# Moving GpSimd's candidate sums of the product-key search to between the two halves of the next head's scores

## The chip, the cores and the metric

The kernel runs on one core of one Trainium2 chip. The metric is the device time of one execution in microseconds (us): the median of three runs before the change is 2715.93 us (2709.26 to 2721.87). A core has TensorE (PE in the profile), VectorE (DVE), ScalarE (ACT), GpSimd (POOL) and SyncE (SP, which here issues most of the DMAs). Each engine works through its own instructions in the order in which they were put there and waits at an instruction whose input is not ready.

## The reference

The program is two transformer blocks on 512 tokens of width 1024. The change lies in the last part of the second block, a memory layer that looks up experts by product keys:

```python
def chunk(xc):
    q = (xc @ wq).reshape(PEER_CHUNK, PEER_HEADS, 2, half)
    s1 = jnp.einsum('chd,hnd->chn', q[:, :, 0], keys1)
    s2 = jnp.einsum('chd,hnd->chn', q[:, :, 1], keys2)
    v1, i1 = lax.top_k(s1, 16)
    v2, i2 = lax.top_k(s2, 16)
    cand = (v1[..., :, None] + v2[..., None, :]).reshape(..., 256)
    cidx = (i1[..., :, None] * 128 + i2[..., None, :]).reshape(..., 256)
    best, pos = lax.top_k(cand, 16)
    eidx = jnp.take_along_axis(cidx, pos, axis=-1)
    g = jax.nn.softmax(best, axis=-1)
    a = jnp.einsum('chkd,cd->chk', u_tab[eidx], xc)
    wgt = gelu(a) * g
    return jnp.einsum('chk,chkd->cd', wgt, v_tab[eidx])
```

Every token has 8 heads. A head has two halves of 128 scores each; the 16 largest of each half are added pairwise, and the 16 largest sums choose 16 of 16,384 experts.

## The kernel before, in words

`peer` (L1395) treats three of the four groups of 128 tokens densely: all 128 blocks of `u_tab` are multiplied with those 384 tokens on TensorE (`u_chunk`, L1422), and the chosen experts' weights are then picked from the result. The fourth group fetches its 128 rows of `u_tab` and `v_tab` per token by indirect DMA (`gather`, L1478; `use`, L1498).

The stage around the change is the search, L1514 to L1612. The loop at L1605 goes over the 8 heads and is one head ahead with its scores: `scores(h + 1)` is called before `best16(h)`.

`scores(h)` (L1522) does the following for each half: it loads a tile of 128x1024 of the query weights and splits it into a high and a low part (`wload`, L72: ScalarE makes the high part at L69, GpSimd the low part at L70); 24 matmuls of 512 columns make the queries (`mm3`, L87 to L89); ScalarE copies them (L1534); four small matmuls with the keys make the scores (L1538), which ScalarE copies to `sk` (L1540); VectorE takes the 16 largest of each of the four token groups with `top16` (L1385: the values at L1388 and L1392 into the tile `tkv`, the indices at L1389 and L1393 into `tki`). Then `ahead(1)` (L1436) puts one `u_chunk` behind it: another split by ScalarE and GpSimd, 24 matmuls of 384 columns, and a Gelu on ScalarE (L1430). Such blocks give TensorE work while VectorE searches.

`best16(h, val, ixu)` (L1546) begins with four GpSimd additions (L1551) that make the 80 candidate sums which can be among the 16 largest (`cand`). VectorE takes their 16 largest (L1557, again `top16`, tile `best`), ScalarE makes the softmax (L1563, L1565), and VectorE turns the positions back into expert indices (the decode, L1576 to L1601, with ScalarE's copies at L1572, L1587, L1599 and L1602). For odd heads, `ahead(h % 2)` adds one more block (L1559). After it the loop calls `gather(2)` from the second head on: GpSimd issues two indirect DMAs (L1493) and multiplies two rows that came earlier (L1503). Before `best16(7)` there are four more blocks, `ahead(TRANS)`, L1608.

What sets the order: for GpSimd, the order of this stage is that of the program text (`manual_schedule`, L1474). For the other engines a scheduler of the framework, which simulates the program as it is written down, chooses the order of instructions. So GpSimd's queue before the change is, for head h of the loop: split of half 0 of head h+1, split of a block, split of half 1 of head h+1, split of a block, the four sums of head h, (odd h: split of a block), two indirect DMAs with two multiplications. The tile `whi` has three buffers, `acc` two, `cand` two, `tkv` three.

Of the kernel before, what the change touches and what calls it, by code (L numbers as in the profile page):

```python
# [9 lines left out]
F32 = mybir.dt.float32  # L10
# [6 lines left out]
ALU = mybir.AluOpType  # L17
# [6 lines left out]
NT = S // 128  # L24
# [22 lines left out]
class Emit:  # L47
# [1347 lines left out]
    def peer(self):  # L1395
        tc, nc, A = self.tc, self.nc, self.A
# [8 lines left out]
        with ExitStack() as es:  # L1405
# [108 lines left out]
            with ExitStack() as ek:  # L1514
                pv = ek.enter_context(tc.tile_pool(name="pval", bufs=1))
                slot = pv.tile([128, 3, ND, 128], F32, name="slot")
                i16 = pv.tile([128, 2, 16], F16, name="i16")
                for half in range(2):
                    nc.gpsimd.iota(i16[:, half], pattern=[[1 + 3 * half, 16]], base=0, channel_multiplier=0,
                                   allow_small_or_imprecise_dtypes=True)  # L1520
                pk = ek.enter_context(tc.tile_pool(name="pk", bufs=2))
                def scores(h):  # L1522
                    val = pk.tile([128, NT, 2, 16], F32, name="tkv", bufs=3)
                    ixu = pk.tile([128, NT, 2, 16], U32, name="tki", bufs=3)
                    keys = pk.tile([128, 256], F32, name="keys")
                    self.dma(keys, A["pkeys"][h])
                    for half in range(2):
                        wh, wl = self.wload(A["pwq"][2 * h + half], eng=nc.gpsimd if h >= 0 else None)
                        ps = self.acc()
                        for k in range(KD):  # L1530
                            c = slice(k * 128, k * 128 + 128)
                            self.mm3(ps, wh[:, c], wl[:, c], hh[:, k], hl[:, k], k == 0, k == KD - 1)
                        q = pk.tile([128, S], F32, name="pq")
                        nc.scalar.activation(q, ps, AF.Copy)  # L1534
                        p3 = self.bank()
                        for t in range(NT):
                            c = slice(t * 128, t * 128 + 128)
                            mm(p3[:, c], lhsT=q[:, c], rhs=keys[:, half * 128:half * 128 + 128], start=True, stop=True)  # L1538
                        sk = pk.tile([128, NT, 128], F32, name="sk")
                        nc.scalar.activation(sk, p3.rearrange("p (t n) -> p t n", t=NT), AF.Copy)  # L1540
                        for t in range(NT):
                            self.top16(pk, sk[:, t], 128, val[:, t, half], ixu[:, t, half])
                        ahead(1)
                    return val, ixu

                def best16(h, val, ixu):  # L1546


                    cand = pk.tile([128, NT, 80], F32, name="cand")
                    for o, i0, ni, nj in BLOCKS:  # L1550
                        nc.gpsimd.tensor_tensor(  # L1551
                            cand[:, :, o:o + ni * nj].rearrange("p t (i j) -> p t i j", i=ni),
                            val[:, :, 0, i0:i0 + ni, None].to_broadcast([128, NT, ni, nj]),
                            val[:, :, 1, None, 0:nj].to_broadcast([128, NT, ni, nj]), op=ALU.add)
                    best = pk.tile([128, NT, 16], F32, name="best")
                    pos = pk.tile([128, NT, 16], U32, name="pos")
                    for t in range(NT):  # L1557
                        self.top16(pk, cand[:, t], 80, best[:, t], pos[:, t])
                    ahead(h % 2)  # L1559
                    g = pk.tile([128, NT, 16], F32, name="gslot")  # L1560
                    mx = pk.tile([128, NT], F32, name="bmx")
                    nm = pk.tile([128, NT], F32, name="bnm")
                    nc.scalar.activation(nm, best[:, :, 0], AF.Copy, scale=-1.0)  # L1563
                    for t in range(NT):
                        nc.scalar.activation(g[:, t], best[:, t], AF.Exp, bias=nm[:, t:t + 1],  # L1565
                                             accum_out=mx[:, t:t + 1])
                    nc.vector.reciprocal(mx, mx)
                    hs = slice(h * 16, h * 16 + 16)
                    tt(slot[:, 2, :, hs], g[:, :ND], mx[:, :ND, None].to_broadcast([128, ND, 16]), op=ALU.mult)
                    tt(gg[:, hs], g[:, ND], mx[:, ND:NT].to_broadcast([128, 16]), op=ALU.mult)  # L1570
                    kf = pk.tile([128, NT, 2, 16], F16, name="kfl")
                    nc.scalar.activation(kf, ixu, AF.Copy)  # L1572


                    u = [pk.tile([128, NT, 16], U32, name=f"pu{i}", bufs=1) for i in range(3)]
                    ts(u[0], pos, 2, 0x3c, op0=ALU.logical_shift_left, op1=ALU.bitwise_and)  # L1576
                    ts(u[0], u[0], 0x40, None, op0=ALU.bitwise_or)
                    ts(u[1], pos, 4, 7, op0=ALU.logical_shift_right, op1=ALU.bitwise_xor)
                    tt(u[2], u[0], u[1], op=ALU.logical_shift_right)
                    tt(u[1], u[2], u[1], op=ALU.logical_shift_left)  # L1580
                    tt(u[0], u[0], u[1], op=ALU.bitwise_xor)
                    ts(u[0], u[0], 0x3c, None, op0=ALU.bitwise_and)
                    e = pk.tile([128, 2, NT, 16], F32, name="e12")
                    for half in range(2):

                        pu = pk.tile([128, NT * 16, 2], F16, name=f"pu2{half}")
                        nc.scalar.activation(pu, (u[0] if half else u[2]).rearrange("p t k -> p (t k)")[:, :, None]  # L1587
                                             .to_broadcast([128, NT * 16, 2]), AF.Copy)
                        eq = pk.tile([128, NT * 16, 16], F16, name="eq", bufs=2)
                        tt(eq.rearrange("p n (i j) -> p n i j", j=2), pu[:, :, None].to_broadcast([128, NT * 16, 8, 2]),  # L1590
                           i16[:, half].rearrange("p (i j) -> p i j", j=2)[:, None].to_broadcast([128, NT * 16, 8, 2]),
                           op=ALU.is_equal)
                        eq4 = eq.rearrange("p (t k) i -> p t k i", t=NT)
                        tt(eq4, eq4, kf[:, :, half, None, :].to_broadcast([128, NT, 16, 16]), op=ALU.mult)

                        for n in (8, 4):
                            tt(eq[:, :, 0:n], eq[:, :, 0:n], eq[:, :, n:2 * n], op=ALU.add)
                        red(e[:, half].rearrange("p t k -> p (t k)"), eq[:, :, 0:4], axis=AX.X, op=ALU.add)
                    nc.scalar.activation(slot[:, 0:2, :, hs], e[:, :, :ND], AF.Copy)  # L1599
                    ef = pk.tile([128, 16], F32, name="ef")  # L1600
                    stt(ef, e[:, 0, ND], 128.0, e[:, 1, ND], op0=ALU.mult, op1=ALU.add)  # L1601
                    nc.scalar.activation(ei[:, hs], ef, AF.Copy)  # L1602

                cur = scores(0)
                for h in range(8):  # L1605
                    nxt = scores(h + 1) if h < 7 else None
                    if h == 7:
                        ahead(TRANS)  # L1608
                    best16(h, *cur)
                    if h:  # L1610
                        gather(2)
                    cur = nxt  # L1612
                for t in range(ND):
                    c = slice(t * 32, t * 32 + 32)
                    p = self.bank()
                    for j in range(3):
                        nc.tensor.transpose(p[:, j * 128:j * 128 + 128], slot[:, j, t], self.ident)
                    v = [p[:, j * 128:j * 128 + 128].rearrange("p (q n) -> p q n", n=4) for j in range(3)]
                    for i in range(2):
                        for j in range(2):  # L1620
                            nc.scalar.activation(eT[:, c, j, :, i], v[j], AF.Copy)
                        nc.scalar.activation(eT[:, c, 2, :, i], v[2], AF.Copy, scale=WSCALE)
                    for i in range(2):
                        stt(eT[:, c, 3, :, i], v[2], WSCALE, eT[:, c, 2, :, i], op0=ALU.mult, op1=ALU.subtract)
# [322 lines left out]
```

## Time and profile before

| | us |
|---|---|
| median of three runs (lowest, highest) | 2715.93 (2709.26, 2721.87) |
| the profiled execution's own time | 2710.84 |
| its span, first to last instruction | 2709.1 |
| the search stage, sums of head 0 to sums of head 7 | 195.7 (1405.7 to 1601.4) |

The span is what the instructions of the profiled execution cover; its own time is 1.7 us longer, for what lies around them. The mean granted TensorE clock of the execution is 0.945 of full speed. All times in the rows below are counted from the span's start.

### The profile page before, as it was taken

The page shows a single profiled execution, that of the slowest core. Times are in us where ns is not written, and L with a number is a line of the kernel's source. Part 1 is how long each engine was busy: PE and PEld are TensorE (multiplying, and loading weights), DVE is VectorE, ACT ScalarE, POOL GpSimd, SP SyncE. Part 2 cuts the span into 40 slices and gives each one's busy share as a digit, 9 for nine tenths or more (in the row PEclk, how much of TensorE's full clock was granted, in tenths as well). Part 3 has the DMA queues.
Part 4 walks back from the last instruction along what each step waited for, and adds up shares of the span by engine and source line. Part 5 has one row for each costly group of instructions (what it writes and reads, how often), then busy time and mean ns, then how long its engine had stood idle before and what let it go on. Part 6 is the DMA issues. An engine that isn't in the chain of part 4 may idle for free.

```text
span 2709.1 us, 33479 instructions
## 1 busy us (share of the span) xinstructions
PE 2445.6 (90%) x11725; PEld 1911.1 (71%) x11725; DVE 1824.4 (67%) x3149; ACT 1090.5 (40%) x1688; POOL 939.3 (35%) x777
## 2 busy tenths in 40 slices
PE   7999897879977988989798889989899999999997
PEld 6776566423335766668587778979688878888886
DVE  6677965334346576564648889977877767767676
ACT  5555434212215336653444554434433333333233
POOL 1002640111100310000145665420676765666661
PEclk9999998889988988999899999989899999999998
DMA  4114684789975211104534448997699988888884
GB/s 143 63 56 170 226 291 159 283 336 391 400 274 212 94 59 47 39 31 144 186 114 136 148 159 305 348 347 276 197 299 301 305 299 266 291 300 284 275 294 152
DMA packets 215934, 589.47 MB, mean 218 GB/s; under 512 B 30565, under 2 KB 85349, under 8 KB 214740
## 3 DMA queue, kind: packets, MB, share of 16 engines
q1 hardware_dynamic: 170836, 433.91, 45.9%
q0 software_dynamic: 44928, 153.42, 16.1%
q8 instruction: 92, 1.51, 0.2%
q14 instruction: 78, 0.64, 0.1%
HBM read 541.85 MB, written 53.78 MB: 220 GB/s over the span
## 4 chain that ended last, share of the span: by engine, by line
PE 30%; DVE 12%; DMA 10%; issue 9%; ACT 4%; POOL 3%; POOLq 0%; SPq 0%; DVEq 0%; ACTq 0%
DMA wraw<-puT 5%; PE acc L87 4%; PE acc L89 4%; PE acc L88 4%; PE yp L87 4%; PE yp L88 4%; PE yp L89 4%; DMA grow<-pvr,ei 3%; POOL grow L1493 2%; DVE wlo L70 2%; DMA gd<-gs 1%; PE bank L87 1%; PE bank L89 1%; PE bank L88 1%; DVE gy L1510 1%
## 5 line engine op out<-in xcount | busy, mean ns | idle before, releaser
L69 ACT ACTIVATE whi<-wraw 128x1024 fp32r<-128x1024 f32 (+1 forms) x290 | 300.0, 1035 | 478.1 <-PE acc L88 164.2
L87 PE MATMUL acc<-hph,whi 128*128 128x384 f32 (+1 forms) x1152 | 404.3, 351 | 20.8 <-ACT ga L1430 19.9
L89 PE MATMUL acc<-hph,wlo 128*128 128x384 f32 (+1 forms) x1152 | 402.6, 350 | 6.5 <-DVE wlo L70 5.6
L88 PE MATMUL acc<-hpl,whi 128*128 128x384 f32 (+1 forms) x1152 | 399.4, 347 | 0.0
L70 DVE TENSOR_TENSOR wlo<-wraw,whi 128x1024 fp32r<-128x1024 f32 (+1 forms) x242 | 294.9, 1220 | 138.4 <-ACT whi L69 136.5
L70 POOL TENSOR_TENSOR wlo<-wraw,whi 128x1024 fp32r<-128x1024 f32 x48 | 115.7, 2416 | 481.4 <-ACT whi L69 468.2
L87 PE MATMUL yp<-vhi,wah 128*128 128x512 f32 x732 | 231.0, 395 | 17.4 <-ACT wah L69 17.4
L87 PEld LDWEIGHTS acc<-hph,whi 128*128 128x128 f32 x1152 | 220.5, 191 | 32.8 <-ACT ga L1430 24.6
L89 PEld LDWEIGHTS acc<-hph,wlo 128*128 128x128 f32 x1152 | 220.2, 191 | 19.5 <-DVE wlo L70 12.1
L88 PE MATMUL yp<-vlo,wah 128*128 128x512 f32 x732 | 231.1, 395 | 0.0
L89 PE MATMUL yp<-vhi,wal 128*128 128x512 f32 x732 | 228.3, 395 | 0.0
L88 PEld LDWEIGHTS acc<-hpl,whi 128*128 128x128 f32 x1152 | 220.5, 191 | 7.1 <-DVE hpl L70 0.2
L1685 POOL TENSOR_TENSOR gw<-gw,ga 128x256 f32<-128x256 f32 x128 | 175.8, 1374 | 137.9 <-DMA ga<-ad 76.7
L1493 POOL DMA_INDIRECT grow<-pu,ei x128 | 151.0, 1179 | 209.4 <-DVE grow L1506 173.3
L70 DVE TENSOR_TENSOR vlo<-wraw,vhi 128x1024 fp32r<-128x1024 f32 x122 | 157.6, 1292 | 93.5 <-ACT vhi L69 93.5
L1493 POOL DMA_INDIRECT grow<-pvr,ei x128 | 177.0, 1383 | 119.4 <-DVE gy L1510 96.3
L69 ACT ACTIVATE wah<-gw 128x384 fp32r<-128x384 f32 x126 | 66.2, 526 | 276.7 <-POOL gw L1686 223.3
L1510 DVE SCALAR_TENSOR_TENSOR gy<-grow,wt,gy 128x1024 f32<-128x1024 f32 x127 | 164.0, 1291 | 16.2 <-DMA grow<-pvr,ei 14.2
L87 PEld LDWEIGHTS yp<-vhi,wah 128*128 128x128 f32 x732 | 139.8, 191 | 47.8 <-ACT wah L69 20.4
L70 DVE TENSOR_TENSOR wal<-gw,wah 128x384 fp32r<-128x384 f32 x126 | 94.1, 747 | 104.2 <-ACT wah L69 103.7
L89 PEld LDWEIGHTS yp<-vhi,wal 128*128 128x128 f32 x732 | 139.6, 191 | 31.1 <-DVE wal L70 1.8
L88 PEld LDWEIGHTS yp<-vlo,wah 128*128 128x128 f32 x732 | 139.6, 191 | 27.7
(671 smaller groups left out, 5154.6 us busy)
## 6 DMA issues: line engine op xcount, KB each, us to landing
wraw<-wgu SPq DMA_DIRECT2D x128, 512.0 KB
wraw<-puT SPq DMA_DIRECT2D x128, 512.0 KB
wraw<-pv SPq DMA_DIRECT2D x128, 512.0 KB
wraw<-wd SPq DMA_DIRECT2D x64, 512.0 KB
aw<-wada SPq DMA_DIRECT2D x48, 512.0 KB
gd<-gs SPq DMA_DIRECT2D x8, 2048.0 KB
gw<-gd SPq DMA_DIRECT2D x128, 128.0 KB
ad<-ga SPq DMA_DIRECT2D x80, 192.0 KB
```

The costliest lines, as they stand in the source:

```text
L69: nc.scalar.activation(hi, src, AF.Copy)
L70: (eng or nc.vector).tensor_tensor(lo, src, f32(hi), op=ALU.subtract)
L87: mm(ps, lhsT=wh, rhs=xh, start=first, stop=False)
L88: mm(ps, lhsT=wh, rhs=xl, start=False, stop=False)
L89: mm(ps, lhsT=wl, rhs=xh, start=False, stop=last)
L1493: nc.gpsimd.indirect_dma_start(out=r, out_offset=None, in_=A["pu" if i < 128 else "pvr"], in_offset=bass.IndirectOffsetOnAxis(ap=ei[:, s:s ...
L1510: stt(gy, r, wt[:, s:s + 1], gy, op0=ALU.mult, op1=ALU.add)
L1685: nc.gpsimd.tensor_tensor(gw[:, :TG], gw[:, :TG], g[:, :TG], op=ALU.mult)
```

## The change

The four additions leave `best16` and become a function `sums(val)`. `scores(h + 1, prev)` calls it with the values of head h after half 0 (its `top16` and its `ahead(1)`), before half 1. For the last head, where no further scores come, the loop calls `sums` itself, and before `ahead(TRANS)`. Nothing is added to or taken from the computation.

```diff
+                def sums(val):
+                    cand = pk.tile([128, NT, 80], F32, name="cand")
+                    for o, i0, ni, nj in BLOCKS:
+                        nc.gpsimd.tensor_tensor(
+                            cand[:, :, o:o + ni * nj].rearrange("p t (i j) -> p t i j", i=ni),
+                            val[:, :, 0, i0:i0 + ni, None].to_broadcast([128, NT, ni, nj]),
+                            val[:, :, 1, None, 0:nj].to_broadcast([128, NT, ni, nj]), op=ALU.add)
+                    return cand
+
-                def scores(h):
+                def scores(h, prev=None):
+                    cand = None
...
                         ahead(1)
-                    return val, ixu
-
-                def best16(h, val, ixu):
-                    cand = pk.tile([128, NT, 80], F32, name="cand")
-                    for o, i0, ni, nj in BLOCKS:
-                        nc.gpsimd.tensor_tensor(
...
+                        if half == 0 and prev:
+                            cand = sums(prev[0])
+                    return (val, ixu), cand
+
+                def best16(h, val, ixu, cand):
                     best = pk.tile([128, NT, 16], F32, name="best")
...
-                cur = scores(0)
+                cur, _ = scores(0)
                 for h in range(8):
-                    nxt = scores(h + 1) if h < 7 else None
-                    if h == 7:
+                    if h < 7:
+                        nxt, cand = scores(h + 1, cur)
+                    else:
+                        cand = sums(cur[0])
                         ahead(TRANS)
-                    best16(h, *cur)
+                    best16(h, *cur, cand)
```

GpSimd's queue after the change is, for head h: split of half 0 of head h+1, split of a block, the four sums of head h, split of half 1 of head h+1, split of a block, (odd h: split of a block), two indirect DMAs with two multiplications. For h = 7 it is: the four sums, four splits of `ahead(TRANS)`, one split, two indirect DMAs with two multiplications.

## Rows read from the trace of the kernel before

**Rows 1.** The page's first part: busy time of each engine, share, instructions.
```profile
PE 2445.6 (90%) x11725; PEld 1911.1 (71%) x11725; DVE 1824.4 (67%) x3149; ACT 1090.5 (40%) x1688; POOL 939.3 (35%) x777
```

**Rows 2.** Windows: busy us and instructions of each engine, granted clock, DMA share, GB/s.
```profile
core 0: us, PE busy (x) PEld busy (x) DVE busy (x) ACT busy (x) POOL busy (x), PEclk, DMA share, GB/s
1460.00:1487.20 27.20, 23.91 (x117) 21.18 (x117) 24.60 (x117) 14.33 (x32) 17.60 (x14) 0.94 0.41 136
1487.20:1516.80 29.60, 25.95 (x128) 23.02 (x127) 24.67 (x117) 14.82 (x33) 19.94 (x14) 0.94 0.45 149
1640.00:2709.10 1069.10, 1011.88 (x5385) 888.73 (x5382) 799.82 (x1035) 392.73 (x569) 578.22 (x494) 0.97 0.83 285
```

**Rows 3.** Waits, 1380 to 1640 us: total us, times, longest.
```profile
POOL wlo L70 <- ACT whi L69: 69.8, 22, 6.2
ACT slot L1599 <- DVE e L1598: 33.3, 8, 6.0
DVE best L1388 <- POOL cand L1551: 27.6, 8, 4.9
ACT pu L1587 <- DVE pu L1579: 26.8, 8, 3.7
PE acc L87 <- ACT ga L1430: 19.0, 9, 3.6
```

**Rows 4.** GpSimd's timeline: start, us, instruction, idle before and its releaser.
```profile
1392.79 2.39 POOL L70 TENSOR_TENSOR wlo<-wraw,whi 128x1024 fp32r<-128x1024 f32 x1 [3.92 <-ACT whi L69]
...
1405.68 1.18 POOL L1551 TENSOR_TENSOR cand<-tkv 128x128 f32<-128x128 f32 x4
...
1525.08 4.74 POOL L70 TENSOR_TENSOR wlo<-wraw,whi 128x1024 fp32r<-128x1024 f32 x2
...
1544.00 1.18 POOL L1551 TENSOR_TENSOR cand<-tkv 128x128 f32<-128x128 f32 x4
...
1579.58 2.42 POOL L1503 TENSOR_TENSOR grow<-grow,htok 128x1024 f32<-128x1024 f32 x1
1581.95 4.72 POOL L70 TENSOR_TENSOR wlo<-wraw,whi 128x1024 fp32r<-128x1024 f32 x2
...
1601.36 1.17 POOL L1551 TENSOR_TENSOR cand<-tkv 128x128 f32<-128x128 f32 x4 [5.68 <-DVE tkv L1392]
```

**Rows 5.** VectorE's timeline at the sums of heads 0, 2, 5 and 7.
```profile
1401.61 0.50 DVE L1392 MAX8 tkv<-mr 128x8 f32<-128x128 f32 x2
...
1406.89 0.67 DVE L1388 MAX8 best<-cand 128x8 f32<-128x80 f32 x4 [4.27 <-POOL cand L1551]
1461.26 0.53 DVE L1388 MAX8 best<-cand 128x8 f32<-128x80 f32 x3 [4.93 <-POOL cand L1551]
1525.47 0.51 DVE L1392 MAX8 tkv<-mr 128x8 f32<-128x128 f32 x2
1525.86 4.02 DVE L1576 TENSOR_SCALAR pu<-pos 128x64 uint32<-128x64 uint32 x1
1602.57 0.53 DVE L1388 MAX8 best<-cand 128x8 f32<-128x80 f32 x3 [0.77 <-POOL cand L1551]
```

**Rows 6.** Groups by line and shape, VectorE, 1380 to 1640 us: busy, mean ns, idle before.
```profile
L1576 DVE TENSOR_SCALAR pu<-pos 128x64 uint32<-128x64 uint32 x8 | 26.9, 3368 | 0.0
L1594 DVE TENSOR_TENSOR eq<-eq,kfl 128x1024 f16<-128x1024 f16 x16 | 25.8, 1636 | 0.0
L1590 DVE TENSOR_TENSOR eq<-pu,i 128x1024 f16<-128x1024 f16 x16 | 10.5, 685 | 0.0
L1578 DVE TENSOR_SCALAR pu<-pos 128x64 uint32<-128x64 uint32 x8 | 1.4, 181 | 0.0
```

**Rows 7.** TensorE's timeline: start of query matmuls, of a block, of key matmuls, and again.
```profile
1386.07 0.48 PE L87 MATMUL acc<-hph,whi 128*128 128x512 f32 x1
...
1391.62 0.33 PE L87 MATMUL acc<-hph,whi 128*128 128x384 f32 x1
...
1395.81 1.05 PE L1538 MATMUL bank<-keys,pq 128*128 128x128 f32 x8
1396.62 0.48 PE L87 MATMUL acc<-hph,whi 128*128 128x512 f32 x1
...
1407.17 0.48 PE L87 MATMUL acc<-hph,whi 128*128 128x512 f32 x1
```

More of the change, by code (lines that the diff above doesn't have):

```diff
@@ L1543, in scores @@
                         ahead(1)
-                    return val, ixu
-                def best16(h, val, ixu):
-                    cand = pk.tile([128, NT, 80], F32, name="cand")
-                    for o, i0, ni, nj in BLOCKS:
-                        nc.gpsimd.tensor_tensor(
-                            cand[:, :, o:o + ni * nj].rearrange("p t (i j) -> p t i j", i=ni),
-                            val[:, :, 0, i0:i0 + ni, None].to_broadcast([128, NT, ni, nj]),
-                            val[:, :, 1, None, 0:nj].to_broadcast([128, NT, ni, nj]), op=ALU.add)
+                        if half == 0 and prev:
+                            cand = sums(prev[0])
+                    return (val, ixu), cand
+                def best16(h, val, ixu, cand):
                     best = pk.tile([128, NT, 16], F32, name="best")
```

## The prediction

> **What bounds the kernel now.** I read the page first: PE is busy 90% of the span and POOL 35% [rows 1], so over the whole kernel TensorE sets the pace. Moving four small POOL instructions matters only where PE isn't kept full. The windows show such a place. In the search stage one head takes 27.2 or 29.6 us; PE is busy 23.9 or 26.0 of these at a granted clock of 0.94, while DVE is busy 24.6 or 24.7, whatever the head's parity [rows 2]. From the sums of head 0 to those of head 7, 195.7 us pass [rows 4], or 28.0 a head.
>
> How long would PE need alone? While it was full, a half's query matmuls took 1391.62 - 1386.07 = 5.55 us, a block 4.19 and the key matmuls 0.81 [rows 7]. A head has two of each, 21.1 us, and every second head one block more, 25.3: a mean of 23.2. DVE's 24.6 is more, so DVE bounds the stage, and it is idle for the remaining 3.4 us of a head.
>
> The list of waits names this idle time: DVE stands before the first maximum of the sums, for POOL's cand, eight times for 27.6 us [rows 3]. Single waits are 4.27, 4.93 and 0.77 us for heads 0, 2 and 7 [rows 5]. POOL is not late because it is full (17.6 or 19.9 us a head [rows 2]), but because of what stands ahead of the sums in its queue: low-part splits, which wait for ACT 69.8 us in all, and ACT in turn stands 33.3 and 26.8 us for DVE's decode [rows 3]. It is a ring: DVE's decode holds ACT, ACT holds POOL's splits, these hold the sums, and the sums hold DVE. PE is held by the same ring, 19.0 us for ACT's Gelu [rows 3].
>
> **The change, part by part.** Instructions: none are added or removed. Four additions, 1.18 us together [rows 4], move in POOL's queue past one query split and one block split. They issue no DMA, and SP's queue is untouched.
>
> *Heads 1 to 6.* The sums no longer wait for the second half's two splits. In the pattern of head 5, the pair of splits at 1525.08 (half 0 of head 6 and its block) ends at 1529.8; the sums stand right behind it in the new order, and run at 1544.00 in the old one [rows 4]: 14.2 us sooner. Their input, the last values of head 5, is done at about 1526 [rows 5], so POOL needn't stop there. DVE's waits at these six heads are 27.6 - 4.27 - 0.77 = 22.5 us [rows 3, 5], and I count them as gone: in that time DVE still has the decode of the head before and the next scores to do. What is late next is DVE itself, with its 24.6 us a head, 1.4 above PE's 23.2.
>
> *Head 0.* In the new order the sums come behind a split that ends at 1395.2 [rows 4], but the values end at about 1402.1 [rows 5]: a new wait of 6.9 us on POOL, with the split of half 1 and a block behind it. The sums would then end at 1403.3 instead of 1406.9, which gives DVE 3.5 of its 4.27 us. The queued split would run from 1403.3 to 1405.7, and PE takes up the next half at 1407.17 [rows 7]: covered by 1.5 us. Without that cover each us is PE's.
>
> *Head 7.* The sums wait for the scores in either order (5.68 us before [rows 4]), so the 0.77 us stays. But four block splits that ran before the sums, from 1581.95, now queue behind them. PE lacks those blocks for a while and makes them up during the decode of head 7, when it waited anyhow; the stage's end hangs on DVE's chain there. I price this at nothing for PE. The cover is that DVE is late at this point; if it were gone, it would cost up to the 4.19 us of a block each, 17 in all.
>
> *What VectorE pays beside GpSimd.* L1576 takes 3368 ns on average, its twin of the same shape, L1578, 181 ns; L1594 takes 1636 ns, and L1590 of the same shape 685 [rows 6]. That is 8 x 3.19 + 16 x 0.95 = 40.7 us more than the twins need. The row at 1525.86 shows why: it ends at 1529.88, with POOL's pair of splits that ended at 1529.82 [rows 4, 5]. These operations stand while POOL computes. This is in DVE's 24.6 us, and the change moves which POOL work meets the decode: before, the decode follows the sums and meets the multiplications and the splits behind them; afterwards it meets the second half's splits, which come singly. From below: all of it goes, -40.7 us, though then PE's floor decides. From above: each head meets one more pair like the one at 1525.08, at the 3.84 us by which 4.02 exceeds the twin's 0.18: 8 x 3.84 = +31 us. I take no change for heads 0 to 6, and for head 7 +4 us, since of the four splits that now fall behind its sums (9.6 us) about half should meet its decode.
>
> The Trainium skill (SBUF — State Buffer, "Who interferes with whom") says that such a VectorE operation and a GpSimd one hold the shared port by turns, each for a whole instruction. By that a meeting costs at most one split, 2.4 us, and the upper bound would be 8 x 2.4 = +19. The trace disagrees: 4.02 us, across two splits [rows 4, 5], so the sum keeps the row's bound.
>
> **Sum.** -22.5 - 3.5 + 4 = -22 us. Against the profiled execution's own 2710.84 this gives 2689; against the median, 5 us higher, 2694. I forecast 2691. After the stage PE is busy 1012 of 1069 us [rows 2], so whatever the stage's end gains, the end of the kernel gains.
>
> **The rivals.**
>
> *A, the gain goes into the port.* The decode still meets as many POOL instructions as before and one split of 2.4 us more a head: +19 us, net -3, about 2708 to 2713; with a pair more a head it is +31, net +9, up to 2725. For it: POOL is busy 65 or 67% of a head [rows 2], and DVE runs into it already. Against it: the second half's splits wait for ACT and come singly.
>
> *B, PE becomes the bound.* The decode meets less POOL work, DVE falls under PE's 23.2 us, and the gain is 7 x (28.0 - 23.2) = 34 us: 2677 to 2682. For it: the run of multiplications and splits that L1576 waits out now lies before the sums. Against it: ACT, in its fixed order, must also let PE through.
>
> *C, slower: POOL stands at the sums.* If the values of head h come after POOL has reached its sums, the second half's split stands behind them and PE runs dry, as it would at head 0 but for 1.5 us. A head then takes PE's 23.2 us plus what isn't covered; it decides from 28.0 - 23.2 = 4.8 us a head. With head 0's 6.9 us uncovered throughout, a head takes 30.1, and seven of them +15 us: 2726 to 2731. For it: POOL obeys the text's order, and a quicker DVE stage brings the sums close to the values. Against it: at head 5 the values are 4 us early.
>
> That the change doesn't do what it says can't be: POOL's order here is the text's.
>
> **How the numbers follow.** My forecast gets 0.46, B 0.17, A 0.24, C 0.13. A difference of 0.5% (about 14 us) is what a measurement of this kernel can tell from no change. The forecast and B lie beyond it: faster 0.63. A lies within it: same 0.24. C is slower by about that: 0.13. The range reaches from B with a few us for a shorter tail, 2674, into A, 2714; it leaves out C, A's pairs and the edges. The forecast's own range is 2682 to 2701.
>
> **What would show it.** Right: DVE's wait for cand drops from 27.6 to under 8 us; the sums of heads 0 and 7 lie about 174 us apart; POOL's wait for tkv stays with heads 0 and 7; L1576 keeps a mean near 3 us. A would show as L1576 and L1594 growing by 19 us together, B as a DVE idle for sk with PE at a clock of 1.0, C as POOL idle before the sums in every head and PE idle behind it. I'm wrong if DVE's wait for cand goes and the stage doesn't shorten, or if it stays.

## The result and the profile after

The changed kernel takes 2735.15 us, the median of six runs (2729.5 to 2740.5), beside 2714.55 for the kernel before: a ratio of 1.0091, with a 95% interval of 1.0074 to 1.0107. The change costs 20.6 us where I forecast a gain of 22. Its profiled execution spans 2729.9 us, 20.8 more than before.

The list of waits of the changed kernel, 1380 to 1660 us, of which these lines are a part, answers to [rows 3] (its L1527 is the sums, L1606 is L1599 of before):

```profile
POOL cand L1527 <- DVE tkv L1392: 66.3, 6, 15.1
ACT slot L1606 <- DVE e L1605: 44.3, 8, 11.8
POOL wlo L70 <- ACT whi L69: 29.3, 13, 5.4
DVE tkv L1388 <- ACT sk L1553: 28.7, 9, 14.1
PE acc L87 <- ACT ga L1430: 25.2, 6, 8.4
POOL cand L1527 <- PE acc L88: 15.3, 2, 8.2
DVE best L1388 <- POOL cand L1527: 6.1, 8, 0.8
```

VectorE's wait for the sums is all but gone, 27.6 to 6.1 us. In its place GpSimd stands ahead of the sums for 66.3 + 15.3 = 81.6 us, where it stood 5.7 before, and TensorE stands 25.2 us behind ScalarE's Gelu instead of 19.0. ScalarE's wait for the end of the decode grew from 33.3 to 44.3 us, but its waits inside the decode (for `pu`) fell from 26.8 + 5.5 to 15.2 + 3.1 us, so that together they are no longer than before. The windows from sums to sums of heads 3, 4 and 5 answer to [rows 2]:

```profile
1488.00:1522.30 34.30, 26.86 (x132) 24.12 (x131) 31.86 (x118) 15.38 (x32) 20.04 (x13) 0.85 0.39 129
1522.30:1553.70 31.40, 26.26 (x125) 23.53 (x124) 29.47 (x118) 14.38 (x31) 17.36 (x13) 0.89 0.36 118
1553.70:1588.00 34.30, 25.91 (x129) 23.38 (x128) 31.85 (x118) 15.60 (x32) 20.03 (x14) 0.85 0.39 125
```

A head takes 31.4 or 34.3 us instead of 27.2 or 29.6, and VectorE, with the same 118 instructions (117 before), is busy 29.5 or 31.9 us instead of 24.6. The granted clock of these windows is 0.85 to 0.89 instead of 0.94, and TensorE is idle for 5.1 to 8.4 us of each. From the sums of head 0 to those of head 7 it is 211.5 us (1404.50 to 1616.04), 15.8 more. VectorE's busy time in between, added over seven such windows, went from 171.6 to 194.3 us (+22.8), and its idle time only from 24.1 to 17.2 (-6.9). So what the stage loses are operations that take longer, not more operations. All of the loss lies behind the sums of head 2. In the windows from the sums of head 0 to those of head 1, and from there to head 2, GpSimd makes no multiplications yet, and the changed order is 1.1 and 1.4 us faster. Before:

```profile
1405.70:1431.20 25.50, 23.81 (x129) 21.42 (x128) 22.64 (x117) 13.39 (x29) 10.73 (x10) 1.00 0.32 104
1431.20:1460.00 28.80, 26.59 (x134) 23.75 (x134) 23.88 (x117) 13.15 (x28) 14.99 (x12) 0.94 0.48 153
```

and after:

```profile
1404.50:1428.90 24.40, 24.40 (x132) 22.46 (x131) 22.97 (x118) 13.63 (x28) 10.82 (x8) 1.00 0.33 108
1428.90:1456.30 27.40, 25.36 (x136) 22.74 (x135) 25.04 (x118) 14.66 (x28) 15.48 (x11) 1.00 0.46 161
```

The groups of VectorE, 1380 to 1640 us, show where most of the longer time went (L1597 was L1590, L1601 was L1594, L1583 was L1576):

```profile
L1597 DVE TENSOR_TENSOR eq<-pu,i 128x1024 f16<-128x1024 f16 x16 | 41.8, 2614 | 0.0
L1601 DVE TENSOR_TENSOR eq<-eq,kfl 128x1024 f16<-128x1024 f16 x16 | 17.7, 1109 | 0.0
L1583 DVE TENSOR_SCALAR pu<-pos 128x64 uint32<-128x64 uint32 x8 | 6.5, 812 | 0.3
```

L1590, which met nothing before (685 ns each [rows 6]), now takes 2614. L1576 fell from 3368 to 812. I use one sum below, *the decode's lines*: the 120 instructions that write pu and eq, added from this view over 1385 to 1680 us. It is 92.5 us before and 109.6 after.

What happens in a head shows in VectorE's timeline from the sums of head 3 to those of head 4 (`...` stands for rows left out: other maxima and index searches, and short operations of the decode):

```profile
1489.24 0.67 DVE L1388 MAX8 best<-cand 128x8 f32<-128x80 f32 x4 [0.76 <-POOL cand L1527]
...
1493.06 0.92 DVE L1583 TENSOR_SCALAR pu<-pos 128x64 uint32<-128x64 uint32 x1
...
1497.40 0.86 DVE L1388 MAX8 tkv<-sk 128x8 f32<-128x128 f32 x4
1498.18 3.35 DVE L1597 TENSOR_TENSOR eq<-pu,i 128x1024 f16<-128x1024 f16 x1
...
1501.98 8.07 DVE L1597 TENSOR_TENSOR eq<-pu,i 128x1024 f16<-128x1024 f16 x1
...
1518.00 0.87 DVE L1388 MAX8 tkv<-sk 128x8 f32<-128x128 f32 x4 [1.54 <-ACT sk L1553]
...
1521.78 0.48 DVE L1392 MAX8 tkv<-mr 128x8 f32<-128x128 f32 x2
...
1523.54 0.68 DVE L1388 MAX8 best<-cand 128x8 f32<-128x80 f32 x4 [0.76 <-POOL cand L1527]
```

and in GpSimd's over the same stretch:

```profile
1488.04 1.17 POOL L1527 TENSOR_TENSOR cand<-tkv 128x128 f32<-128x128 f32 x4 [5.20 <-DVE tkv L1392]
1489.17 4.76 POOL L70 TENSOR_TENSOR wlo<-wraw,whi 128x1024 fp32r<-128x1024 f32 x2
...
1502.41 2.40 POOL L1503 TENSOR_TENSOR grow<-grow,htok 128x1024 f32<-128x1024 f32 x1
1504.77 4.73 POOL L70 TENSOR_TENSOR wlo<-wraw,whi 128x1024 fp32r<-128x1024 f32 x2
1522.34 1.17 POOL L1527 TENSOR_TENSOR cand<-tkv 128x128 f32<-128x128 f32 x4 [12.84 <-DVE tkv L1392]
```

One operation of the decode, at 1501.98, stands until GpSimd's multiplication and two splits are over (1509.50) and ends 0.55 us behind them. All that follows it on VectorE is late: the rest of the decode, then the values of the second half of head 4, at 1521.78, and only then can GpSimd make the next sums. The order on VectorE is new too, but for the first half only. Before, the first half's values of the next head came beside the maxima of the sums and ahead of the decode (1525.47 and 1525.86 in [rows 5]: head 5's first half, then the decode of head 4); now they come inside the decode (from 1497.40). The second half's values come behind most of the decode in both kernels; in the kernel before, those of head 5 are these:

```profile
1536.86 0.86 DVE L1388 MAX8 tkv<-sk 128x8 f32<-128x128 f32 x4
...
1541.75 0.50 DVE L1392 MAX8 tkv<-mr 128x8 f32<-128x128 f32 x2
```

That they are head 5's can be counted: the 8 heads have 16 halves, and this is the twelfth stretch of four maxima `tkv<-sk` of 16 that the trace of before has. ScalarE's and TensorE's timelines of the changed kernel show the rest of the ring:

```profile
1515.68 0.28 ACT L1606 ACTIVATE slot<-e 128x96 f32<-128x96 f32 x1 [10.87 <-DVE e L1605]
1515.87 0.47 ACT L1430 ACTIVATE ga<-acc 128x384 f32<-128x384 f32 x1
```

```profile
1516.40 0.80 PE L87 MATMUL acc<-hph,whi 128*128 128x512 f32 x1 [7.44 <-ACT ga L1430]
```

ScalarE stands 10.87 us for the decode, TensorE 7.44 us for the Gelu behind it. When the decode of head 7 ends, TensorE has been busy for 197.8 us since the first values of head 0, where it was 209.4 before, and what follows takes 1098.0 us instead of 1086.1.

### The profile page after: what moved, and what is told of

Its sections match the earlier page's. It is cut to its first block, busy times and chain, and to the rows that moved or that the text cites. A ratio compares the mean times of both kernels' runs of the same rounds, so it can differ in the third digit from the quotient of the medians.

```text
span 2729.9 us, 33456 instructions
## 1 busy us (share of the span) xinstructions
PE 2445.8 (90%) x11725; PEld 1912.3 (70%) x11725; DVE 1853.8 (68%) x3149; ACT 1091.8 (40%) x1690; POOL 921.7 (34%) x777
## 3 DMA queue, kind: packets, MB, share of 16 engines
q0 software_dynamic: 44928, 153.42, 15.8%
## 5 line engine op out<-in xcount | busy, mean ns | idle before, releaser
L1493 POOL DMA_INDIRECT grow<-pvr,ei x128 | 170.7, 1334 | 118.1 <-DVE gy L1510 96.5
L1694 POOL TENSOR_TENSOR gw<-gw,ga 128x256 f32<-128x256 f32 x128 | 151.7, 1185 | 141.4 <-DMA ga<-ad 64.0
```

The costliest lines, as they stand in the source:

```text
L1493: nc.gpsimd.indirect_dma_start(out=r, out_offset=None, in_=A["pu" if i < 128 else "pvr"], in_offset=bass.IndirectOffsetOnAxis(ap=ei[:, s:s ...
L1694: nc.gpsimd.tensor_tensor(gw[:, :TG], gw[:, :TG], g[:, :TG], op=ALU.mult)
```

## The experiments

I told three theories apart. PORT: the decode's operations stand while GpSimd computes. WAIT: GpSimd stands at the sums and holds the next half's split. TAIL: the last head's order. A fourth, ORDER, came later: VectorE decodes one head ahead of the next head's values. In the diffs `...` stands for lines left out. Differences are those of medians against the kernel before, timed in the same sessions.

**Which heads.** `e1` is the kernel before with only the last head's order changed:

```diff
+                    cand = sums(cur[0])
                     if h == 7:
                         ahead(TRANS)
-                    best16(h, *cur)
+                    best16(h, *cur, cand)
```

> The kernel before, with only the last head's order changed: its four sums stand ahead of the four blocks of ahead(TRANS) in GpSimd's queue; heads 0 to 6 are as before. Three theories for the 21 us that the change lost. PORT (VectorE's decode stands at the port that it shares with GpSimd for the whole of GpSimd's run of splits and multiplications): no change to +5 us against before. WAIT (GpSimd stands at the sums until VectorE has the head's values, and the next half's split stands behind them): only the last head is hit, 0 to +6 us. TAIL (the last head's order is what costs): +12 to +20 us.

2719.78 us, +7.3 (ratio 1.0028, 1.0013 to 1.0042): above what PORT and WAIT had, and below what TAIL had. `e2` is the changed kernel with the last head put back:

```diff
+                        ahead(TRANS)
                         cand = sums(cur[0])
-                        ahead(TRANS)
```

> The changed kernel with the last head's order put back (ahead(TRANS), then the sums); heads 0 to 6 keep the sums between the halves. PORT and WAIT: still slower than before by 12 to 21 us, with the sums of heads 0 to 6 as far apart as in the changed kernel (183 us from the sums of head 0 to those of head 6). TAIL: no slower than before, 2695 to 2718 us.

2726.18 us, +13.7 (1.0047, 1.0027 to 1.0068). The two add up to the change: about a third is the last head, and two thirds are heads 0 to 6. Their price shows in the search: from the first values to the last operation of head 7's decode the profiled execution takes 253.4 us, where the kernel before takes 235.7.

**GpSimd's stand taken away.** `e3` leaves the right candidates out, so that the sums wait for no values but head 0's:

```diff
-                        nxt, cand = scores(h + 1, cur)
+                        nxt, cand = scores(h + 1, old)
...
-                        cand = sums(cur[0])
+                        cand = sums(old[0])
...
-                    cur = nxt
+                    old, cur = cur, nxt
```

> The changed kernel, but the sums of head h add the values of head h-1, which are long there (head 0 adds its own): GpSimd's order is kept, and its stand at the sums goes. This leaves out the right candidates: the sums belong to the wrong head. WAIT: GpSimd's 82 us idle before the sums go to under 15, and the time falls below that of before, to 2680 to 2705 us. PORT: VectorE's collisions stay (L1597 above 2 us on average, VectorE busy about 190 us from the sums of head 0 to those of head 7), and the time stays at 2725 us or more.

2728.14 us, +15.7 (1.0049, 1.0031 to 1.0067). GpSimd's stand is gone but for head 0's 7.0 us; the decode's lines are still 103.7 us, and ScalarE stands longer for the end of the decode than in the changed kernel:

```profile
ACT slot L1606 <- DVE e L1605: 56.7, 8, 9.0
POOL cand L1527 <- PE acc L88: 7.0, 1, 7.0
```

Not all is as PORT had it: L1597 fell to 1098 ns, and L1601 (1748) and the additions behind it grew in its place. `e6` takes the sums off GpSimd altogether:

```diff
-                        nc.gpsimd.tensor_tensor(
+                        nc.vector.tensor_tensor(
                             cand[:, :, o:o + ni * nj].rearrange("p t (i j) -> p t i j", i=ni),
```

> The changed kernel with its four sums on VectorE instead of GpSimd: nothing on GpSimd waits for the values any more, and VectorE waits for no sums. WAIT: the 82 us that GpSimd stood go, the half's split is never held, and the time falls to 2690 to 2710. PORT: GpSimd's splits and multiplications come as densely as before or more so, the decode meets them, and the time stays at 2720 us or above.

2725.31 us, +14.4 (1.0045, 1.0024 to 1.0066). The time is still lost with no sums on GpSimd, but VectorE has the sums to make now, 11.0 us, so this says less than `e3`. In its groups the meetings lie at other lines of the decode, 97.9 us in all:

```profile
L1601 DVE TENSOR_TENSOR eq<-eq,kfl 128x1024 f16<-128x1024 f16 x16 | 32.7, 2066 | 0.0
L1589 DVE TENSOR_SCALAR pu<-pu 128x64 uint32<-128x64 uint32 x8 | 15.5, 1943 | 0.1
```

WAIT falls as the cause of most of the price: with the stand gone, 15.7 of the 20.6 us stay. What the other 5 are is not separated.

**GpSimd's work taken away.** `e4`, `e5` and `e9` are the changed kernel, the kernel before and `e2`, each with

```diff
-GPOOL = 16
+GPOOL = 0
```

> The changed kernel with GPOOL = 0: the 14 multiplications of 2.4 us that GpSimd makes in this stage (34 us) go to VectorE as one operation of about 1.2 us each (17 us), so that no run of two multiplications and two splits stands on GpSimd any more. PORT: L1597 falls from 2614 ns to under 1500 on average, VectorE's work shrinks by some 30 us in collisions and grows by 17, and the time falls by 8 to 20 us from the changed kernel's, to 2715 to 2727. WAIT: the values come no sooner, VectorE has 17 us more to do, and the time stays or grows, 2735 to 2750 us.

2705.94 us, 6.5 under before (0.998, 0.9965 to 0.9994), so 27 less than the changed kernel's +20.6 and more than PORT had, though VectorE has the kernel's 16 multiplications more (16 and not 14, as the trace of before counts them at L1503; 10 of them lie between the sums of head 0 and those of head 7 there). GpSimd still stands 86.7 us at the sums; L1597 is at 1136 ns:

```profile
POOL cand L1527 <- DVE tkv L1392: 79.7, 7, 14.7
POOL cand L1527 <- PE acc L88: 7.0, 1, 7.0
```

```profile
L1597 DVE TENSOR_TENSOR eq<-pu,i 128x1024 f16<-128x1024 f16 x16 | 18.0, 1136 | 0.0
```

> The kernel before with GPOOL = 0 (the control to the changed kernel with GPOOL = 0, which ran 6.5 us under before): the 14 multiplications of the stage on VectorE. PORT, with the long run of multiplications and splits as the cause: the old order loses little to that run (L1576 and L1594), so it gains less from its going than the 29 us of the changed kernel, and lands at 2695 to 2710; the change's price of 21 us shrinks to under 10. If the price of the change were independent of GpSimd's work (WAIT): the same 29 us gain, about 2685, and the price stays at 21.

2697.52 us, 13.4 under before (0.996, 0.9944 to 0.9976): about half of the changed kernel's gain. The whole change costs about 7 us here instead of 21. The gain of the old order doesn't lie in the search, which takes 239.6 us (235.7 before), but behind it: from the end of head 7's decode to the end, 1064.0 us instead of 1086.1. No run separates why.

> Heads 0 to 6 in the changed order, the last head in the old one, and GPOOL = 0 (no multiplications on GpSimd). PORT: the price of the changed order for heads 0 to 6, 14 us with the multiplications, is their meeting with the decode and is gone without them: within 5 us of the kernel before with GPOOL = 0, 2692 to 2703 us. WAIT: the price stays, 2707 to 2716 us.

2694.37 us, 16 under before (0.9937, 0.992 to 0.9954). Beside `e5` the changed order of heads 0 to 6 now costs nothing, with GpSimd still standing 72 us at the sums. The search takes 235.2 us here and 239.6 in `e5`, where with the multiplications on GpSimd the same step, from the kernel before to `e2`, was 235.7 to 253.4. The 14 us that the order costs otherwise are thus made by the multiplications on GpSimd together with it; the 10 us by which `e4` lies above `e9` are the last head's (7.3 in `e1`).

**The order alone.** `e11` leaves three of the four additions where the change put them and takes the fourth back behind both halves; the last head is in the old order:

```diff
-                def sums(val):
...
+                def sums(val, blocks=BLOCKS, cand=None):
...
-                            cand = sums(prev[0])
+                            cand = sums(prev[0], BLOCKS[:3])
+                    if prev:
+                        sums(prev[0], BLOCKS[3:], cand)
...
+                        ahead(TRANS)
                         cand = sums(cur[0])
-                        ahead(TRANS)
```

> Three of a head's four sums between the halves, as in the changed kernel, and the fourth behind both halves, as before; the last head in the old order. GpSimd must stand at the first three until the values are there, but VectorE's maxima and decode can only follow the fourth, as late as before. ORDER (a third theory: the early sums let the scheduler put the decode of head h ahead of the second half's values of head h+1 on VectorE and ScalarE, so that the search loses its lead of a head, and the decode meets GpSimd's run): no difference from before, within 5 us. WAIT: GpSimd's stand alone holds the second half's split; 8 us or more slower than before. PORT without ORDER: no difference from before either.

2708.48 us, -2.0: no difference (0.9994, 0.9979 to 1.001). GpSimd stands at the early sums of heads 0 to 6, 7 to 11 us each, and that costs nothing:

```profile
1483.25 0.92 POOL L1526 TENSOR_TENSOR cand<-tkv 128x128 f32<-128x128 f32 x3 [11.35 <-DVE tkv L1392]
...
1488.79 0.32 POOL L1526 TENSOR_TENSOR cand<-tkv 128x64 f32<-128x64 f32 x1
```

On VectorE the first half's maxima of the next head are back beside those of the sums and ahead of the decode:

```profile
1489.13 0.53 DVE L1388 MAX8 best<-cand 128x8 f32<-128x80 f32 x3 [0.82 <-POOL cand L1526]
...
1493.13 0.47 DVE L1392 MAX8 tkv<-mr 128x8 f32<-128x128 f32 x2
...
1495.29 0.20 DVE L1584 TENSOR_SCALAR pu<-pos 128x64 uint32<-128x64 uint32 x1
```

An operation of the decode behind these rows still stands for 7.76 us. WAIT, which had 8 us or more, falls here too. ORDER had no difference, but so had PORT: the decode's lines are 84.0 us here, less than before, so this run doesn't tell the two apart. ORDER alone isn't the price, for `e9` has the changed order and costs nothing. And what I had written of ORDER holds for the first half only: the second half's values lie behind the decode in the kernel before as well.

**Other places on GpSimd.** `e7` puts the sums behind the second half's split, `e8` the gathers behind the sums, `e10` the query splits on VectorE:

```diff
+                        if half == 1 and prev:
+                            cand = sums(prev[0])
...
-                        if half == 0 and prev:
-                            cand = sums(prev[0])
```

> The changed kernel with the sums of heads 0 to 6 one place later in GpSimd's queue: behind the query split of the second half, ahead of its block's split. The split that was held no longer is, one split less stands between the sums and GpSimd's multiplications. WAIT: PE gets its second half in time and the time falls by 10 us or more, to 2710 to 2725. PORT: the run ahead of the sums is one split longer, VectorE stands no shorter, and the time stays at 2728 to 2742 us.

2735.17 us, +24.2 (1.0087, 1.0068 to 1.0107), as PORT had it: freeing the second half's split wins nothing.

```diff
                             cand = sums(prev[0])
+                            if h > 1:
+                                gather(2)
...
-                    if h:
+                    if h == 7:
                         gather(2)
```

> The changed kernel with the two indirect DMAs and multiplications of heads 1 to 6 moved in GpSimd's queue: from behind the head's last split to right behind the head's sums. They then run while VectorE takes the maxima of the sums, which stand at no port, and the run ahead of the next sums is 7 us shorter. PORT: the 8 us meetings of L1597 go, the decode's lines fall from 110 us to under 95, and the time falls by 8 to 25 us from the changed kernel's, to 2710 to 2727. WAIT: the second half's split comes 7 us later behind the sums in each head, and the time grows by 10 us or more, to 2745 and above.

2740.29 us, +29.4 (1.0109, 1.0086 to 1.0131): neither PORT's number nor WAIT's came. I had meant the multiplications to pass while VectorE takes maxima; but the three splits queue up behind them, and the first operations of the decode stand for the whole run:

```profile
1496.42 2.36 POOL L1503 TENSOR_TENSOR grow<-grow,htok 128x1024 f32<-128x1024 f32 x1
1498.72 6.99 POOL L70 TENSOR_TENSOR wlo<-wraw,whi 128x1024 fp32r<-128x1024 f32 x3
```

```profile
L1586 DVE TENSOR_SCALAR pu<-pu 128x64 uint32<-128x64 uint32 x8 | 42.2, 5271 | 0.0
```

The decode's lines are 100.1 us, less than the changed kernel's, and yet the time is longer; the splits for TensorE also come 7 us later. Which share is whose was not separated.

```diff
-                        wh, wl = self.wload(A["pwq"][2 * h + half], eng=nc.gpsimd if h >= 0 else None)
+                        wh, wl = self.wload(A["pwq"][2 * h + half], eng=None)
```

> The changed kernel with the 16 query splits (low part, 2.4 us each on GpSimd) on VectorE, 1.2 us each; the block splits and multiplications stay on GpSimd. PORT: GpSimd has 38 us less to hold the port with, VectorE 19 us more to do; the decode's lines fall from 110 us to under 95 and the time to 2712 to 2730. WAIT: the second half's split no longer stands behind the sums, so PE runs ahead, and the time falls below that of before, under 2710 us.

2725.88 us, +15.4 (1.0051, 1.0036 to 1.0066): 5 us less than the changed kernel's +20.6, with the decode's lines at 85.2 us. That is within PORT's numbers; VectorE has 16 splits more to make, and a split takes it 1.56 us on average there.

**Both.** `e12` is `e11` with GPOOL = 0.

> Three of a head's four sums early, the fourth late, the last head in the old order, and GPOOL = 0. If GpSimd's multiplications are what turns the order into a price, all three orders cost the same without them: 2690 to 2702 us, with the kernel before at 2697.5 and the changed order of heads 0 to 6 at 2694.4. If the order has a price of its own, this one, whose decode met GpSimd least with the multiplications in place, is the fastest by 8 us or more, under 2688.

2706.44 us, -4.1 (0.9987, 0.9973 to 1.0001): it was neither the fastest nor level with `e5` and `e9`. Why it lies 9 and 12 us above them stays open; its profiled execution, 2698.66 us, is the fastest of its ten, so its trace shows little of it. Taking the multiplications off GpSimd is worth 2 us in this order and 13 in the old one, so they are not the whole account.

## Why the prediction was wrong

- **"Their input, the last values of head 5, is done at about 1526 [rows 5], so POOL needn't stop there"** is the first step that failed, and the row was misread. The values that end at 1526 are those of head 5's first half. Its last values end at 1542.25 (the row at 1541.75 above). So head 5's sums, at 1544.00, followed them by 1.8 us, and a place that GpSimd reaches at 1529.8 meant a stand of 12.4 us there. The changed kernel has such a stand in every head: 7.0 us for head 0, 5.2 to 12.8 for heads 1 to 6, 15.1 for head 7.
- **"I count them as gone"** came for the wait itself (27.6 to 6.1 us) but not for the time: VectorE's idle time in the stage fell by 6.9 us. It waits elsewhere now, for scores (28.7 us instead of 19.9) and for ScalarE's part of a split (7.9 instead of 1.1).
- **"I take no change"** for what VectorE pays beside GpSimd is the term that turned the sign: it was put at 0, and VectorE's busy time between the sums grew by 22.8 us; the decode's lines grew by 17.1. My reason, that the second half's splits come singly, was wrong. Behind GpSimd's stand they came as a pair (4.76 us at 1489.17), and the later half of the decode met a multiplication and a pair of splits, in the row above for 8.07 us. `e2` and `e9` show that this price needs the multiplications on GpSimd. Whether it comes from the stand, which packs GpSimd's work behind it, or from the place of the first half's values on VectorE is not separated; that the scheduler would choose again for VectorE stood in no step of mine. Rival A had this price (+19, or +31 by pairs) but kept the 22 us of gain beside it.
- **Rival C** named the sign, the place (+15 us, 30.1 us a head; it is 30.2) and the rows (GpSimd idle before the sums in every head), and its condition was met in the trace of before already: my point against it, "at head 5 the values are 4 us early", rests on the misread row. Still the stand alone isn't the cause: without it (`e3`) three quarters of the loss stay, and with it (`e9`, `e11`) there is none. The size agreed by accident.
- **The sign of being wrong** that I had named came: VectorE's wait for `cand` goes and the stage doesn't shorten.
- **Head 0** came as worked out: its sums lie 3.5 us earlier behind the first maxima (18.4 to 14.9 us), and nothing was lost by GpSimd's 7.0 us there: TensorE is busy for all 24.40 us up to the sums of head 1.
- **Head 7**: I took +4 us, for its decode meeting the splits behind the sums, and nothing for TensorE's blocks; `e1` gives +7.3 (3.5 to 11.4 by its interval). The size is near, but by luck. In `e1` the decode's lines are shorter than before (80.7 us, not 92.5). GpSimd stands 11.8 us at these sums with the blocks' splits behind it, and when head 7's decode ends, TensorE has been busy for 193.1 us instead of 209.4: the term put at nothing is the one that shows.
- **The port's rule.** The Trainium skill (SBUF — State Buffer, "Who interferes with whom") says that a VectorE operation with two inputs in SBUF contends with a GpSimd operation that reads SBUF, and that whichever is issued first has the shared ports for its whole instruction while the other waits. The trace agrees with the first: L1597 has two such inputs and stands. From the second I had worked out a price of one instruction at most, and that doesn't hold here: 8.07 us span one multiplication and two splits. The bound from the row was right to stand in the sum.

## What to carry to other kernels

A row that is to show an input ready must be of the input's last part: here a head's values come in two stretches, and counting them up to the row would have shown the stand that the change makes. Where VectorE's operations stand for GpSimd's, long runs on GpSimd are a cost of VectorE's chain: the changed order of heads 0 to 6 made the search 17.7 us longer with the multiplications on GpSimd, and no longer without them. With the multiplications on VectorE, which makes one in about half the time (1.28 us beside 2.41), the old order and the changed order of heads 0 to 6 both beat the kernel before, by 13 and 16 us; for the old order the gain lies behind the search. And an idle engine next to the moved work need not be the cause: take the idle time away alone before believing it.

## What was not expected of the hardware

A single VectorE operation of 0.69 us stood for 8.07 us behind three GpSimd instructions that followed each other without a gap; one of 0.2 us stood for 7.76 in `e11`, and another for 9.16 in `e8`, behind a multiplication and three splits. In these rows a meeting costs the rest of GpSimd's run, not the rest of its current instruction.
